# A hybrid attention and MoE block: fourteen instead of twelve column blocks of W_in beside the first norm's modulation

## The chip, the cores and the metric

The kernel runs on one core of a Trainium2 chip, all in float32. The time is the device time of one execution in microseconds (us); lower is better. Engines are named as the profile names them: PE (TensorE, with PEld for its weight loads), DVE (VectorE), ACT (ScalarE), POOL (GpSimd) and SP (SyncE, which here only issues loads).

## The reference

One layer on 256 tokens of width 2048, with a conditioning vector c:

```
mod = silu(c) @ w_ada + b_ada                  # sh1, sc1, gt1, sh2, sc2, gt2, 2048 wide each
h = modulate(rms_norm(x, g_mix), sh1, sc1)
qa, ka, va, qb, kb, vb = split(h @ w_in)       # 1024, 256, 256, 1024, 1024, 1024 columns
o_a = sliding-window attention of 16 heads (4 key heads, ALiBi, sinks)
o_b = chunked attention of 16 heads with a learned relative bias
x = x + gt1 * (concat(rms_norm(o_a), rms_norm(o_b)) @ w_out)
h = modulate(rms_norm(x, g_ffn), sh2, sc2)
x = x + gt2 * hier_moe(h)                      # 4 groups of 8 experts, top 1 group, top 2 experts
y = modulate(rms_norm(x, g_final), shf, scf)   # from silu(c) @ w_ada_final
```

All weights together are some 595 MB, read once.

## The kernel before

**The ring.** Every large weight goes through one ring of six buffers of 2 MB (`RING = 6`, class `Ring`). SP issues the loads in one fixed order. The load of a tile is issued when a buffer is free, so at most six tiles are on their way, waiting, or in use.

**First stage (four quarters q).** Quarter q holds four tiles of w_ada, 2 MB each (columns of sh1 and sc1), and two tiles of W_in's first 1536 columns, 1.5 MB each (`first_quarters`). PE does the w_ada products of quarter 0 and of the fourth tile of the other quarters (L314); DVE does the first three tiles of quarters 1 to 3 (L319, L321). The sums are transposed into columns (L329 to L338), the four chunks of hT are modulated (L342, L344), and then PE multiplies the chunks by ten blocks of 128 columns (qA and kA, L349) and by vA's 256 columns (L354). They add up over the quarters in six PSUM banks (`early`, `early_v`). One more PSUM bank ("m") and two of tag "t", which take the modulation sums and all transposes in turn, fill the eight.

**Second stage (`in_step`).** The remaining 3072 columns of W_in are six blocks of 512 columns: qB0, kB0, vB0, qB1, kB1, vB1. Each is two tiles of 8 chunks, so there are 12 steps of 2 MB (L575, L579). Between the PE tiles lie "vector tiles" in the ring: 2 MB of w_ada or w_ada_final, which DVE alone multiplies by silu(c) and adds up in four instructions each (`vec_step`, L383, L385). `VECTOR_TILES` says how many of the 44 lie behind each PE tile: 2 and 3 in turn over the twelve steps.

**Attention.** `weave(n)` is called twice per step: it starts the next n heads (`scores`: PE products, DVE maxima L475 and L476, ACT exponentials, DVE reciprocals L493, POOL scaling L494 and L495), transposes the heads of the call before (`turn`, L502) and multiplies those of the call before that by the values (`values`, L518). After each of a head's four phases it emits up to two instructions of vector tiles, if any are queued. The 16 heads of A come first. POOL makes a bias tile for each of them (L462).

**The order on each engine** is that in which the program emits instructions. The loop over the tiles is

```
    step = out_step(h, idx) if name == "wo" else in_step(name, h, idx)
    next(step)
    queue += [(*tile, kk) for tile in extra for kk in range(tile[2])]
    vec_steps(4)
    for _ in step:
        pass
    vec_steps()
```

`in_step` yields after each half of its tile: after the first half `weave(0)` has been called, after the second `weave(2)`.

**Third stage (`out_step`).** Eight tiles of w_out (L608): four for A's half, then, when all heads are through and B's norm (L536) is known, four for B's half, with the router between. `weave(1 + t)` is called after each of an A step's two token halves, so three heads can start in one step. Then 8 passes over four experts each take the 192 tiles of the MoE through the same ring (L819, L847).

Of the kernel before, what the change touches and what calls it, by code (L numbers as in the profile page):

```python
# [18 lines left out]
AF = mybir.ActivationFunctionType  # L19
# [16 lines left out]
NEG = -1e30  # L36
RING = 6

VECTOR_TILES = [2, 3, 2, 3, 2, 3, 2, 3, 2, 3, 2, 3, 2, 2, 2, 2, 3, 2, 1, 0]


ROW_ADA, ROW_FIN, ROW_MIX, ROW_FFN, ROW_GFIN, ROW_OA, ROW_OB = 0, 24, 32, 36, 40, 44, 46
# [42 lines left out]
def block_kernel(ctx: ExitStack, tc: tile.TileContext, a: dict):  # L85
# [7 lines left out]
    ring = Ring(nc, ringp, RING)  # L93
# [5 lines left out]
    def rows(w, row, n, col, width):  # L99

        return w[row : row + 128 * n, col : col + width].rearrange("(k p) n -> p k n", p=128)
# [3 lines left out]
    first_quarters = []  # L105
    for q in range(4):
        gemv = [ring.add((4, 2, 512), [rows(ada, 512 * i, 4, s * D + q * 512, 512) for s in range(2)]) for i in range(4)]
        first_quarters.append((gemv, [ring.add((2, 1536), rows(w_in, q * 512 + h * 256, 2, 0, 1536)) for h in range(2)]))

    vec_tiles = []  # L110
    for name, w, col in (("gt1", ada, 2 * D), ("sh2", ada, 3 * D), ("sc2", ada, 4 * D), ("gt2", ada, 5 * D), ("scf", fin, D), ("shf", fin, 0)):
        for c in (0,) if name == "shf" else (0, 1024):
            vec_tiles += [((name, c // 512), k, 4, 1024, rows(w, k * 512, 4, col + c, 1024)) for k in range(4)]
    blocks = [("qB0", 1536), ("kB0", 2560), ("vB0", 3584), ("qB1", 2048), ("kB1", 3072), ("vB1", 4096)]
    pe_tiles = [(name, h, rows(w_in, h * 1024, 8, col, 512)) for name, col in blocks for h in range(2)]
    pe_tiles += [("wo", h * 4 + n, rows(w_out, h * 1024, 8, n * 512, 512)) for h in range(2) for n in range(4)]
    order = []
    for (name, h, src), count in zip(pe_tiles, VECTOR_TILES):
        part = ring.add((8, 512), src)
        extra = [(vn, k, n, ring.add((n, width), vs)) for vn, k, n, width, vs in vec_tiles[:count]]  # L120
        del vec_tiles[:count]
        order.append((name, h, part, extra))
# [88 lines left out]
    with ExitStack() as sa:  # L211
# [4 lines left out]
        def bank(tag, name, bufs=2):  # L216
            return ps.tile([128, 512], F32, tag=tag, name=name, bufs=bufs)

        pc = bank("m", "pc", 1)
        PE.transpose(pc[:, 0:16], crow, ident[0:16, 0:16])  # L220
        ce = pa.tile([128, 16], F32, name="ce")
# [22 lines left out]
        G.dma_start(out=U, in_=rel[:, 0:UW])  # L244


        p0 = bank("t", "p0")
        p1 = bank("t", "p1")
        for q in range(4):
            PE.transpose(p0[:, q * 128 : (q + 1) * 128], pr[:, q * 128 : (q + 1) * 128], ident)  # L250
        for q in range(4):
# [49 lines left out]
        kS = bflat[:, 1024:1536].rearrange("p (c n) -> p c n", c=2)  # L301
        R["gt1"] = bflat[:, 3584:4096]
        for q, (gemv, parts) in enumerate(first_quarters):
            mods = bank("t", f"mods{q}")
            on_vector = gemv[:3] if q else []
            acc = pa2.tile([128, 1024], F32, tag="acc", name=f"acc_first{q}").rearrange("p (s n) -> p s n", s=2) if q else None
            for i, idx in enumerate(gemv):
                w = ring.get(idx)
                for k in range(4):
                    c = cact[:, 4 * i + k : 4 * i + k + 1]  # L310
                    if idx not in on_vector:
                        for s in range(2):
                            r = 64 * s + 32 * (k % 2)
                            PE.matmul(  # L314
                                mods[r : r + 32, :], lhsT=c.to_broadcast([128, 32]), rhs=w[:, k, s, :],
                                start=i == len(on_vector) and k < 2, stop=i == 3 and k > 1 and not (q and k == 2), skip_group_check=True,
                            )
                    elif i or k:
                        V.scalar_tensor_tensor(acc, w[:, k], c, acc, op0=ALU.mult, op1=ALU.add)  # L319
                    else:  # L320
                        V.tensor_scalar(acc, w[:, k], c, None, op0=ALU.mult)  # L321
                ring.release(idx)
                if q == 0 and i == 1:
                    turn_x()
                    early = [bank("w", "qA0"), bank("w", "qA1"), bank("s", "qA2"), bank("s", "qA3"), bank("v", "kA", 1)]
                    early_v = bank("m", "vA", 1)
            if q:
                for s in range(2):
                    PE.matmul(mods[64 * s : 64 * s + 32, :], lhsT=ones[:, 0:32], rhs=acc[:, s], start=False, stop=True, skip_group_check=True)  # L329
            row = oT_flat[:, 2048 + (q % 2) * 512 : 2560 + (q % 2) * 512]  # L330
            S.copy(row, mods)
            pt = bank("t", f"mod{q}")
            for c in range(4):
                PE.transpose(pt[:, c * 128 : (c + 1) * 128], row[:, c * 128 : (c + 1) * 128], ident)
            cols = small.tile([128, 2, 4], F32, tag="mod", name=f"mod{q}")
            V.tensor_reduce(cols, pt.rearrange("p (c s h r) -> p s c h r", c=4, s=2, h=2)[:, :, :, :, 0], axis=AX.X, op=ALU.add)
            V.tensor_tensor(cols, cols, bmod[:, :, q, :], op=ALU.add)
            V.tensor_tensor(cols[:, 1, :], cols[:, 1, :], gmix[:, q, :], op=ALU.mult)  # L338
            for c in range(4):
                k = 4 * q + c  # L340
                if c % 2:
                    S.activation(hT[:, k, :], hT[:, k, :], AF.Identity, bias=cols[:, 0, c : c + 1], scale=cols[:, 1, c : c + 1])  # L342
                else:
                    V.tensor_scalar(hT[:, k, :], hT[:, k, :], cols[:, 1, c : c + 1], cols[:, 0, c : c + 1], op0=ALU.mult, op1=ALU.add)  # L344
            for c in range(4):
                kk = 4 * q + c
                w = ring.get(parts[c // 2])[:, c % 2, :]
                for n in range(10):
                    PE.matmul(  # L349
                        early[n // 2][:, (n % 2) * 256 : (n % 2 + 1) * 256], lhsT=w[:, n * 128 : (n + 1) * 128], rhs=hT[:, kk, :],  # L350
                        start=kk == 0 and n % 2 == 0, stop=kk == 15, skip_group_check=True,
                    )
                for t in range(2):
                    PE.matmul(  # L354
                        early_v[:, t * 256 : (t + 1) * 256], lhsT=hT[:, kk, t * 128 : (t + 1) * 128], rhs=w[:, 1280:1536],
                        start=kk == 0 and t == 0, stop=kk == 15, skip_group_check=True,
                    )
                if c % 2:
                    ring.release(parts[c // 2])
# [3 lines left out]
        for s in range(4):  # L363
# [3 lines left out]
            else:  # L367
                V.tensor_scalar(dst, early[s], 0.125, None, op0=ALU.mult)
        V.tensor_copy(vA.rearrange("p t n -> p (t n)"), early_v)


        accs = {}
# [124 lines left out]

        def turn(kind, h):
            st = live.pop((kind, h))
            tp = bank("t", f"tp{kind}{h}")  # L500
            for i in range(3):
                PE.transpose(tp[:, i * 128 : (i + 1) * 128], st[:, i * 128 : (i + 1) * 128], ident)  # L502
            pt = pa2.tile([128, 384], F32, tag="pt", name=f"pt{kind}{h}")
            S.copy(pt, tp[:, 0:384])
            live["T", kind, h] = pt
# [59 lines left out]

        def in_step(name, h, idx):
            w = ring.get(idx)
            if h == 0:
                open_banks["b"] = [bank("w", f"pw_{name}{i}") for i in range(2)]
            b = open_banks["b"]  # L570
            for s in range(2):
                for k in range(8):
                    kk = 8 * h + k
                    if name[0] == "v":
                        PE.matmul(b[s], lhsT=hT[:, kk, s * 128 : (s + 1) * 128], rhs=w[:, k, :], start=kk == 0, stop=kk == 15)  # L575
                    else:
                        for n in range(2):
                            c = 2 * s + n
                            PE.matmul(  # L579
                                b[s][:, n * 256 : (n + 1) * 256], lhsT=w[:, k, c * 128 : (c + 1) * 128], rhs=hT[:, kk, :],  # L580
                                start=kk == 0 and n == 0, stop=kk == 15, skip_group_check=True,
                            )
                if s == 1:
                    ring.release(idx)
                if h == 1:
                    if name[0] == "v":
                        S.copy(half[name][:, s, :], b[s])
                    else:
                        dst, scale = dest[name]
                        S.activation(dst[:, 2 * s : 2 * s + 2, :].rearrange("p c n -> p (c n)"), b[s], AF.Identity, scale=scale)  # L590
                weave(2 * s)
                yield
# [32 lines left out]

        def router_turns(n):
            for c in range(2):
                tp = bank("t", f"x1t{n}{c}")
                hh = hflat[:, D + 1024 + c * 512 : D + 1024 + (c + 1) * 512].rearrange("p (j n) -> p j n", j=2)
                for j in range(2):  # L630
                    for t in range(2):
# [463 lines left out]
```

## Time and profile before

| what | value |
|---|---|
| median of 3 runs | 1508.13 us (1502.47, 1508.13, 1508.76) |
| profiled execution | 1504.53 us, its span 1502.9 us |
| PE / DVE / ACT / POOL busy | 79% / 33% / 11% / 10% of the span |
| moved from memory | 599.38 MB, mean 399 GB/s |
| mean granted PE clock | 0.913 of full speed |

The span runs from the first to the last instruction; 1.6 us of the profiled execution lie outside it. Busy time of PE is modelled, and shares are means over stages with different limits, so the stages have to be read one by one.

### The profile page before, as it was taken

To read this page: it belongs to the slowest core of one execution; us is meant where nothing else is said; L and a number is where in the kernel's file an instruction comes from. 1 tells how busy PE (TensorE), PEld (TensorE's weight loads), DVE (VectorE), ACT (ScalarE), POOL (GpSimd) and SP (SyncE) were. 2 spreads that over 40 slices of the span, in tenths; PEclk is the share of its full clock that TensorE was granted. 3 is DMA by queue.
4 is the path that set the end of the run, shared out by engine and by line. 5 is a ranking of instruction groups with operands and counts; after the bars stand their busy time and mean duration, and the time that the engine had idled before them with its cause. 6 is when DMAs were issued, how large, how long until landed. Compare 5 with 4: busy or idle time off the path is not lost.

```text
span 1502.9 us, 14247 instructions
## 1 busy us (share of the span) xinstructions
PE 1190.7 (79%) x5927; PEld 528.7 (35%) x5928; DVE 495.8 (33%) x803; ACT 167.4 (11%) x425; POOL 155.1 (10%) x144
## 2 busy tenths in 40 slices
PE   5898999999999987766677667767767757666877
PEld 2676875864444532222212212211211211221222
DVE  1453688877668520111111211111201201111113
ACT  2000222223221210000000100000100000000012
POOL 1000245532441100000000000000000000000002
PEclk9899999999999998889879989888989988898998
DMA  9999999999888999999999999999999999999995
GB/s 335 395 393 400 383 402 402 402 401 401 339 325 321 385 390 421 421 419 421 421 422 421 421 421 421 421 422 421 421 421 421 421 421 421 421 421 421 421 410 182
DMA packets 125469, 599.38 MB, mean 399 GB/s; under 512 B 5880, under 2 KB 8488, under 8 KB 78040
## 3 DMA queue, kind: packets, MB, share of 16 engines
q1 hardware_dynamic: 121248, 594.82, 98.0%
q10 hardware_dynamic: 4120, 3.57, 0.7%
q8 instruction: 48, 0.79, 0.2%
q14 instruction: 21, 0.17, 0.0%
q0 software_dynamic: 32, 0.02, 0.0%
HBM read 596.02 MB, written 2.12 MB: 398 GB/s over the span
## 4 chain that ended last, share of the span: by engine, by line
DMA 45%; PE 10%; DVE 0%; issue 0%; ACT 0%; ACTq 0%; SPq 0%; DVEq 0%
DMA ring<-w_up 22%; DMA ring<-w_down 12%; DMA ring<-w_gate 12%; PE up L819 4%; PE yp L847 3%; PE gp L819 2%; PE sc_g L866 1%; PE last L1050 0%; PE last L1049 0%; ACT big L1061 0%; DVE ys_g L860 0%; PE last L1060 0%; ACTq L1062 0%; DVE act_g L836 0%; PE sm_g L810 0%
## 5 line engine op out<-in xcount | busy, mean ns | idle before, releaser
L847 PE MATMUL yp<-ring,actT_g 128*32 128x512 f32 x1024 | 186.2, 784 | 102.9 <-DMA ring<-w_down 97.1
L819 PE MATMUL up<-ring,xg_g 128*32 128x512 f32 x1024 | 171.6, 701 | 78.2 <-DMA ring<-w_up 78.2
L819 PE MATMUL gp<-ring,xg_g 128*32 128x512 f32 x1024 | 169.2, 692 | 62.7 <-DMA ring<-w_gate 61.4
L868 DVE TENSOR_TENSOR x<-x,sc_g 128x512 f32<-128x512 f32 x64 | 44.0, 688 | 255.4 <-PE sc_g L866 255.4
L847 PEld LDWEIGHTS yp<-ring,actT_g 128*32 128x32 f32 x1024 | 40.0, 135 | 233.8 <-DMA ring<-w_down 135.2
L608 PE MATMUL po<-ring,oT 128*128 128x512 f32 x256 | 116.1, 609 | 0.5 <-DMA ring<-w_out 0.5
L789 DVE TENSOR_SCALAR xg_g<-g_g,gsc,sh2c 128x128 f32<-128x128 f32 x64 | 26.2, 409 | 257.9 <-PE g_g L780 240.6
L871 POOL TENSOR_TENSOR big<-x,xg_gscf 128x512 f32<-128x512 f32 x8 | 10.0, 1273 | 960.9 <-DVE x L868 960.9
L819 PEld LDWEIGHTS up<-ring,xg_g 128*32 128x32 f32 x1024 | 38.1, 124 | 197.5 <-DMA ring<-w_up 111.7
L819 PEld LDWEIGHTS gp<-ring,xg_g 128*32 128x32 f32 x1024 | 37.2, 122 | 180.5 <-DMA ring<-w_gate 90.4
L787 ACT ACTIVATE xg_g<-g_g,sh2c,gsc 128x128 f32<-128x128 f32 x64 | 29.3, 457 | 511.6 <-DVE xg_g L789 509.6
L860 DVE TENSOR_TENSOR ys_g<-yp,gt2bc 128x512 f32<-128x512 f32 x32 | 21.8, 690 | 174.1 <-PE yp L847 174.1
L385 DVE SCALAR_TENSOR_TENSOR acc_gt<-ring,cact,acc_gt 128x1024 f32<-128x1024 f32 x60 | 78.5, 1309 | 1.6
L608 PEld LDWEIGHTS po<-ring,oT 128*128 128x128 f32 x256 | 49.1, 196 | 61.3 <-issue 59.8
L780 PEld LDWEIGHTS g_g<-pn_g,big 128*128 128x128 f32 x512 | 59.6, 192 | 28.0 <-issue 27.2
L349 PE MATMUL qA<-hT,ring 128*128 128x256 f32 x256 | 64.6, 410 | 4.8 <-DVE hT L344 3.5
L780 PE MATMUL g_g<-pn_g,big 128*128 128x128 f32 x512 | 65.6, 281 | 1.4 <-DVE pn_g L772 1.4
L866 PE MATMUL sc_g<-ys_g,smat_g 128*128 128x512 f32 x128 | 64.6, 628 | 1.6 <-DVE ys_g L860 1.6
L349 PEld LDWEIGHTS qA<-hT,ring 128*128 128x128 f32 x256 | 52.7, 207 | 14.2 <-DVE hT L344 4.3
L579 PE MATMUL pw_kB<-hT,ring 128*128 128x256 f32 x256 | 57.0, 382 | 0.0
L575 PE MATMUL pw_vB<-ring,hT 128*128 128x512 f32 x128 | 56.5, 597 | 0.0
L579 PE MATMUL pw_qB<-hT,ring 128*128 128x256 f32 x256 | 56.5, 381 | 0.0
(328 smaller groups left out, 1126.6 us busy)
## 6 DMA issues: line engine op xcount, KB each, us to landing
ring<-w_gate SPq DMA_DIRECT2D x64, 2048.0 KB, 20.3
ring<-w_up SPq DMA_DIRECT2D x64, 2048.0 KB
ring<-w_down SPq DMA_DIRECT2D x62, 2048.0 KB, 22.0
ring<-w_ada SPq DMA_DIRECT2D x32, 2048.0 KB, 15.8
ring<-w_ada SPq DMA_DIRECT2D x32, 1024.0 KB, 14.1
ring<-w_ada_final SPq DMA_DIRECT2D x16, 2048.0 KB, 10.9
ring<-w_in SPq DMA_DIRECT2D x12, 2048.0 KB, 16.3
ring<-w_out SPq DMA_DIRECT2D x8, 2048.0 KB
```

The source lines that it names most:

```text
L349: PE.matmul(early[n // 2][:, (n % 2) * 256 : (n % 2 + 1) * 256], lhsT=w[:, n * 128 : (n + 1) * 128], rhs=hT[:, kk, :], start=kk == 0 and n ...
L385: V.scalar_tensor_tensor(accs[name], w[:, kk, :], cact[:, c : c + 1], accs[name], op0=ALU.mult, op1=ALU.add)
L575: PE.matmul(b[s], lhsT=hT[:, kk, s * 128 : (s + 1) * 128], rhs=w[:, k, :], start=kk == 0, stop=kk == 15)
L579: PE.matmul(b[s][:, n * 256 : (n + 1) * 256], lhsT=w[:, k, c * 128 : (c + 1) * 128], rhs=hT[:, kk, :], start=kk == 0 and n == 0, stop=kk = ...
L608: PE.matmul(b, lhsT=oT[:, (i // 4) * 8 + k, t * 128 : (t + 1) * 128], rhs=w[:, k, :], start=k == 0, stop=k == 7)
L780: PE.matmul(pm[:, i * 128 : (i + 1) * 128], lhsT=big[:, t, kk * 128 : (kk + 1) * 128], rhs=pn[:, t, :], start=t == 0 and i == 0, stop=t == ...
L787: S.activation(xg[:, kk, :], pm[:, i * 128 : (i + 1) * 128], AF.Identity, bias=sh2c[:, kk : kk + 1], scale=gsc2[:, kk : kk + 1])
L789: V.tensor_scalar(xg[:, kk, :], pm[:, i * 128 : (i + 1) * 128], gsc2[:, kk : kk + 1], sh2c[:, kk : kk + 1], op0=ALU.mult, op1=ALU.add)
L819: PE.matmul(bankt[32 * e : 32 * e + 32, :], lhsT=xg[:, kk, 32 * e : 32 * e + 32], rhs=w[e // 2][:, e % 2, j, :], start=kk == 0, stop=kk == ...
L847: PE.matmul(y[32 * e : 32 * e + 32, :], lhsT=aT[:, fc, 32 * e : 32 * e + 32], rhs=w(e)[:, n * 512 : (n + 1) * 512], start=fc == 0, stop=fc ...
L866: PE.matmul(pm, lhsT=sm[:, t * 128 : (t + 1) * 128], rhs=ys[:, n, :], start=True, stop=True)
L868: V.tensor_tensor(x1[:, t, c], x1[:, t, c], pm, op=ALU.add)
```

## The change

The two W_in tiles of each quarter become 1792 columns wide (1.75 MB), and PE multiplies each chunk by two more blocks: columns 1536 to 1791, which are the first half of qB0. Their sums stand in a seventh bank, "t1"; the modulation sums of this stage use "t0" alone, and later transposes take t0 and t1 in turn (`tbank`). The other half of qB0 is one tile of 16 chunks of 256 columns (rows of 1 KB), done in one step that has one `weave(2)` and one yield at its end. So there are 11 steps in place of 12, and `VECTOR_TILES` gives them 3, 3, 2 in turn.

```diff
-VECTOR_TILES = [2, 3, 2, 3, 2, 3, 2, 3, 2, 3, 2, 3, 2, 2, 2, 2, 3, 2, 1, 0]
+VECTOR_TILES = [3, 3, 2, 3, 3, 2, 3, 3, 2, 3, 3, 2, 2, 2, 2, 3, 2, 1, 0]
...
-        first_quarters.append((gemv, [ring.add((2, 1536), rows(w_in, q * 512 + h * 256, 2, 0, 1536)) for h in range(2)]))
+        first_quarters.append((gemv, [ring.add((2, 1792), rows(w_in, q * 512 + h * 256, 2, 0, 1792)) for h in range(2)]))
...
-    blocks = [("qB0", 1536), ("kB0", 2560), ("vB0", 3584), ("qB1", 2048), ("kB1", 3072), ("vB1", 4096)]
-    pe_tiles = [(name, h, rows(w_in, h * 1024, 8, col, 512)) for name, col in blocks for h in range(2)]
+    blocks = [("kB0", 2560), ("vB0", 3584), ("qB1", 2048), ("kB1", 3072), ("vB1", 4096)]
+    pe_tiles = [("qB0", 0, rows(w_in, 0, 16, 1792, 256))]
+    pe_tiles += [(name, h, rows(w_in, h * 1024, 8, col, 512)) for name, col in blocks for h in range(2)]
...
-        part = ring.add((8, 512), src)
+        part = ring.add((16, 256) if name == "qB0" else (8, 512), src)
...
+        def tbank(name):
+            turns[0] += 1
+            return bank(f"t{turns[0] % 2}", name, 1)
...
-            mods = bank("t", f"mods{q}")
+            mods = bank("t0", f"mods{q}", 1)
...
+                    early_b = bank("t1", "qB", 1)
...
-            pt = bank("t", f"mod{q}")
+            pt = bank("t0", f"mod{q}", 1)
...
-                for n in range(10):
+                for n in (*range(10), 12, 13):
                     PE.matmul(
-                        early[n // 2][:, (n % 2) * 256 : (n % 2 + 1) * 256], lhsT=w[:, n * 128 : (n + 1) * 128], rhs=hT[:, kk, :],
+                        (early + [None, early_b])[n // 2][:, (n % 2) * 256 : (n % 2 + 1) * 256], lhsT=w[:, n * 128 : (n + 1) * 128], rhs=hT[:, kk, :],
...
+        S.activation(oT[:, 8:10, :].rearrange("p c n -> p (c n)"), early_b, AF.Identity, scale=0.125)
...
-            tp = bank("t", f"tp{kind}{h}")
+            tp = tbank(f"tp{kind}{h}")
...
             w = ring.get(idx)
+            if name == "qB0":
+                b = bank("w", "pw_qB0")
+                for kk in range(16):
+                    for n in range(2):
+                        PE.matmul(
+                            b[:, n * 256 : (n + 1) * 256], lhsT=w[:, kk, n * 128 : (n + 1) * 128], rhs=hT[:, kk, :],
+                            start=kk == 0 and n == 0, stop=kk == 15, skip_group_check=True,
+                        )
+                ring.release(idx)
+                S.activation(half[name][:, 2:4, :].rearrange("p c n -> p (c n)"), b, AF.Identity, scale=0.125)
+                weave(2)
+                yield
+                return
```

## Rows read from the trace of the kernel before

**Rows 1.** The page, section 4: the chain that ended last, by engine.

```profile
DMA 45%; PE 10%; DVE 0%; issue 0%; ACT 0%; ACTq 0%; SPq 0%; DVEq 0%
```

**Rows 2.** Windows: length, engines' busy us (instructions), granted PE clock, DMA share, GB/s.

```profile
45.00:130.00 85.00, 77.08 (x355) 59.05 (x355) 48.37 (x51) 5.03 (x9) 0.00 (x0) 0.96 1.04 395
...
128.80:134.00 5.20, 5.16 (x16) 4.23 (x17) 0.31 (x1) 0.67 (x2) 0.00 (x0) 0.67 1.05 390
...
213.00:361.00 148.00, 148.00 (x660) 94.70 (x658) 118.65 (x201) 41.23 (x127) 60.49 (x53) 1.00 1.03 402
361.00:546.00 185.00, 173.44 (x615) 81.37 (x614) 122.55 (x211) 36.94 (x104) 53.18 (x45) 0.97 0.91 353
666.00:1447.00 781.00, 552.12 (x3056) 166.66 (x3059) 118.53 (x182) 35.26 (x73) 0.00 (x0) 0.88 1.01 421
```

**Rows 3.** Timeline of PE, first stage: start, length in us, ..., [idle before <-releaser].

```profile
49.38 3.62 PE L349 MATMUL qA<-hT,ring 128*128 128x256 f32 x16
...
54.56 3.62 PE L349 MATMUL qA<-hT,ring 128*128 128x256 f32 x16
...
65.01 1.92 PE L314 MATMUL mods<-ring,cact 128*32 128x512 f32 x16
...
70.31 5.41 PE L349 MATMUL qA<-hT,ring 128*128 128x256 f32 x16 [1.19 <-DVE hT L344]
...
92.92 1.04 PE L314 MATMUL mods<-ring,cact 128*32 128x512 f32 x2
...
99.52 3.72 PE L349 MATMUL qA<-hT,ring 128*128 128x256 f32 x16 [1.18 <-DVE hT L344]
...
119.48 1.03 PE L354 MATMUL vA<-ring,hT 128*128 128x256 f32 x4
...
123.52 1.49 PE L314 MATMUL mods<-ring,cact 128*32 128x512 f32 x11 [1.59 <-DMA ring<-w_ada]
...
128.84 5.41 PE L349 MATMUL qA<-hT,ring 128*128 128x256 f32 x16 [1.18 <-DVE hT L344]
```

**Rows 4.** Timeline of PE, second stage.

```profile
151.36 13.98 PE L579 MATMUL pw_qB<-hT,ring 128*128 128x256 f32 x64
...
181.65 14.08 PE L579 MATMUL pw_kB<-hT,ring 128*128 128x256 f32 x64
195.66 0.66 PE L518 MATMUL opA<-ptA,big 128*64 128x256 f32 x4
...
198.14 7.17 PE L579 MATMUL pw_kB<-hT,ring 128*128 128x256 f32 x32
```

**Rows 5.** Timeline of DVE, start of the second stage.

```profile
152.94 6.57 DVE L385 SCALAR_TENSOR_TENSOR acc_gt<-ring,cact,acc_gt 128x1024 f32<-128x1024 f32 x5
168.02 0.29 DVE L475 CUSTOM_DVE_ANT_0 stA<-spA,biasA 128x128 f32<-128x128 f32 x1 [8.50 <-POOL biasA L462]
...
169.77 2.60 DVE L385 SCALAR_TENSOR_TENSOR acc_gt<-ring,cact,acc_gt 128x1024 f32<-128x1024 f32 x2
...
172.73 0.17 DVE L493 RECIPROCAL denA<-denA 128x2 f32<-128x2 f32 x1
```

**Rows 6.** Timeline of POOL, the same stretch.

```profile
166.84 0.20 POOL L454 MEMSET biasB<- 64x128 f32 x1 [3.11 <-DMA biasB<-scratch]
```

**Rows 7.** Loads: KB each, us from issue to landing.

```profile
ring<-w_ada SPq DMA_DIRECT2D x32, 2048.0 KB, 15.8
...
x<-x SPq DMA_DIRECT2D x1, 2048.0 KB, 8.4
```

**Rows 8.** Timeline of PE, third stage.

```profile
361.65 7.13 PE L608 MATMUL po<-ring,oT 128*128 128x512 f32 x16 [0.50 <-DMA ring<-w_out]
...
452.94 0.71 PE L536 MATMUL pnB<-ones,sqB 128*128 128x1 f32 x4 [3.11 <-POOL sqB L529]
```

**Rows 9.** Waits of PE between 350 and 460 us: total us, times, longest.

```profile
PE tpB L502 <- POOL stB L495: 2.1, 4, 0.6
PE tpB L502 <- POOL stB L494: 2.1, 2, 1.5
```

More of the change, by code (lines that the diff above doesn't have):

```diff
@@ L217, in bank @@
             return ps.tile([128, 512], F32, tag=tag, name=name, bufs=bufs)
+        turns = [0]
+        def tbank(name):
+            turns[0] += 1
+            return bank(f"t{turns[0] % 2}", name, 1)
         pc = bank("m", "pc", 1)
@@ L244, in block_kernel @@
         G.dma_start(out=U, in_=rel[:, 0:UW])
-        p0 = bank("t", "p0")
-        p1 = bank("t", "p1")
+        p0 = tbank("p0")
+        p1 = tbank("p1")
         for q in range(4):
@@ L627, in router_turns @@
             for c in range(2):
-                tp = bank("t", f"x1t{n}{c}")
+                tp = tbank(f"x1t{n}{c}")
                 hh = hflat[:, D + 1024 + c * 512 : D + 1024 + (c + 1) * 512].rearrange("p (j n) -> p j n", j=2)
```

## The prediction

> **What bounds the kernel now.** I read the chain of the page first, then the windows by stage, then the timelines of PE and DVE where the change sits. The chain puts 45% of the span on loads and 10% on PE [rows 1], but it is followed back from the end and lies in the MoE almost wholly, so the earlier part must be read from the windows. From 666 us to 1447 us loads run at 421 GB/s and PE has slack [rows 2]: whatever delays the start of the MoE is added to the end, for its 192 tiles can hardly come faster. From 361 to 546 us PE is busy 173.4 of 185 us and loads fall to 353 GB/s: PE sets the pace, and the ring is full behind it. From 45 to 361 us both are nearly full: loads at 395 to 402 GB/s, PE 77.1 of 85 us in the first stage and 148 of 148 in most of the second [rows 2]. Which of the two decides shows where they meet: PE starts the first w_out product at 361.65 us after waiting 0.50 us for its load [rows 8]. So that load's landing is one fixed post, and what PE still owes behind it is the other. My sum goes by these two.
>
> **First stage.** Each of 16 chunks gets two more blocks, four instructions. A chunk is 24 instructions and its pitch is 54.56 - 49.38 = 5.18 us [rows 3], so 64 more cost 64 x 0.216 = 13.8 us, 3.45 us in a quarter. Against that, loads grow by 0.524 MB in a quarter, 1.33 us at 395 GB/s [rows 2]. PE thus falls behind its loads by 2.1 us more in each quarter, and its waits on them go. From the end of one quarter's W_in work to the next one's start PE took 70.31 - 65.01 = 5.3 us where loads were in time, 99.52 - 92.92 = 6.6 and 128.84 - 120.5 = 8.3 where they were late [rows 3]; the last two fall to 5.3, which gives back 4.3 us. The stage's end moves from 151.36 to 151.36 + 13.8 - 4.3 = 160.9 us. Unknown is where the clock falls: one quarter began its W_in work with 16 products in 3.72 us, two with 5.41 [rows 3], behind a wait and at a granted clock of 0.67 [rows 2]; so +/- 1.8 us.
>
> **qB0's rest.** 64 instructions in place of 128: 14.0 us [rows 4], to 174.9 us. One pair of heads less has been started by then; a pair's whole turn (values, transposes, scores) costs PE 198.14 - 195.66 = 2.5 us [rows 4], a debt that is paid later. The scores that are left here I put at a third of it, 0.9 us. So kB0 starts at 175.8, against 181.65 [rows 4]: 5.9 us earlier.
>
> Rows of 1 KB in its load, 7 KB instead of 6 KB before it: loads run at 395 GB/s where rows of 2 KB prevail and at 421 with the MoE's 8 KB [rows 2]. If halving the rows once more cost as much again, this one tile would take 0.3 us longer; PE comes to it late anyway, so I count nothing. The Trainium skill (DMA: Bandwidth & Descriptors, Specifications) puts line rate at transfers of 512 B and more, by which the tile would lose nothing; no run here shows rows of 1 KB, and its rule alone doesn't explain 395 against 421.
>
> **The vector tiles behind qB0 are where I expect the loss.** Before, the step yields after half a tile, the loop then queues the vector tiles and emits four DVE instructions ahead of the first heads' maxima. The trace shows this order kept: products of the first two tiles from 152.94 us on, then DVE stands idle for 8.50 us until POOL's bias, and the two products that were emitted behind the maxima come only at 169.77, behind them [rows 5]. The new step yields only after weave(2). So the maxima and reciprocals of heads 0 and 1 are emitted ahead of every vector tile, and weave's own vec_steps find an empty queue. DVE does nothing on the ring until those heads are through.
>
> When is that? Before, the first maximum ran 168.02 - 151.36 = 16.7 us after the stage's end [rows 4, 5], held by POOL, which waited for the bias's load until 166.84 [rows 6]. The same distance gives 160.9 + 16.7 = 177.6 us; bounded below by the scores alone, 175.9. From there to the last reciprocal it took 172.9 - 168.0 = 4.9 us with 2.6 us of vector products between [rows 5]; without them between 2.3 and 4.9, I take 3.6. So the first vector tile starts at 181.2, not near 152, and ends four products of 1.3 us [rows 5] later, at 186.4.
>
> Meanwhile the ring fills: qB0, its three vector tiles, kB0's first tile and one more vector tile take the six buffers. The next load waits for qB0's release at 174.9, the one behind it for the first vector tile, 186.4. With the queue run dry a 2 MB load takes 8.4 us, as that of x did alone [rows 7] (least 5.2, a tile at 402 GB/s; most 15.8, the median of w_ada's 2 MB loads in a full queue [rows 7]): it lands at 194.8. From this tile to the first of w_out I count 34 tiles of 2.097 MB in the new order, 5.22 us each at 402 GB/s: 177.5 us. It lands at 372.3 instead of 361.65, **+10.7 us**. Nothing between can make that up, since loads run at their rate already. PE doesn't hold it back: ten steps from 175.8 at the old pace (361.65 - 181.65 = 180.0 us) end at 355.8.
>
> Bounds: scores in place of the bias, 2.3 us, and a load of 5.2 us give 188.6 and +4.4 us; the slower clock (+1.8), 4.9 us and 15.8 us give 205.3 and +21.1. (The Trainium skill's same page, Anatomy of one DMA, fits 2.0 us plus bytes at 436 GB/s to a load issued by POOL; taken over as an estimate that is 6.8 us for such a tile, and the sum would be 1.6 us less. The 8.4 us of x disagree, and stand.)
>
> **Third stage.** PE is the bound, so what it owes adds: the pair of heads, 2.5 us. The heads now end in the fourth w_out step instead of the third, so one pair more is transposed right behind a 7 us block, and waits for POOL as such pairs do: 4.2 us in two places [rows 9], so 0 to 2.1, I take 1.1. Before B's half the last head's values follow its transposes directly, with ACT's copy between, some 0.6 us; the wait for B's norm, 3.11 us [rows 8], was there before. Together **+4.2 us**, at most 7 with one more fall of the clock. Bank turns, the extra ACT copy and wider tiles cost nothing: one copy of 0.6 us on an engine that is 11% busy, and t0 and t1 alternate as the two buffers did.
>
> **Sum.** 1504.5 + 10.7 + 4.2 = 1519.4 us against the profiled execution, with 1511 to 1533 as this case's own range. The three runs lie 2.1 us below to 4.2 us above that execution; for that I add 1.5 us: 1521.
>
> **Rivals.** (1) The hole stays hidden: DVE's tiles are taken up earlier than I read, or the loads queued cover it. Then w_out still lands at 361.65, since its bytes ahead are the same, and only the third stage's debt stays: 1507 to 1510. For it: the median load stood 15.8 us in its queue [rows 7]; against it: six buffers are all there is, and DVE's 8.50 us idle with work behind it. (2) Not slower: PE was the bound all along and the 0.50 us at 361 us chance. Then the 5.9 us count, less the 2.5: -3.4, 1501 us; with the 2.5 us covered too 1499. It decides only if the loads from 45 to 361 us gain 2% (5.9 of 317 us); their share is at 1.03 to 1.04 of the engines already [rows 2], so I doubt it. (3) Worse: DVE, 29 us late, stays late for the heads too, PE's transposes wait in each of ten steps and the clock falls 1.8 us with some of these waits; with 1 us each more, +12 on top: 1533.
>
> **Chances.** My case 0.60, rival 1 0.14, rival 2 0.12, rival 3 0.14. About 0.5%, 7.5 us, is what a measurement of this kernel can tell from none. I count half of rival 2 as faster, for what its two numbers may be short of: 0.06. Same is its other half, rival 1, and a tenth of my case at its low end: 0.26. Slower is the rest of my case and rival 3: 0.68. The range 1506 to 1534 leaves out rival 2 and the upper part of rival 3.
>
> **What will show it.** PE's first stage ends near 161 us and kB0 starts near 176 (wrong if 165: no waits were won back). DVE has no vector product between the stage's end and 180 us, and loads fall well below 395 GB/s between 165 and 195 us; if they don't, my main step is wrong. Between 200 and 372 us PE waits for W_in's tiles. The first w_out product starts near 372 us, and the MoE's first some 15 us later than before. Wrong would make it above all that the loads' gap is shorter than 11 us, or that PE has more room in the third stage than its busy share says.

## The result, and the profile after

The changed kernel takes 1525.34 us, median of five runs (1521.42 to 1528.21), against 1508.13 us, median of five (1502.47 to 1509.59): 1.0124 times the time of before, 95% interval 1.0104 to 1.0144. Ratios here and below are estimated from the runs of both kernels and are not quotients of the medians, which here would give 1.0114. It is slower by 17 us where 13 were forecast. Of all runs in this document one was in a slow state and is left out of its kernel's ratio: 2123.78 us, of x6 below, whose nine others took 1496.54 to 1500.61. The profiled execution is the slowest of its five runs (1528.21 us, span 1526.6); that of before lies 3.6 us under its own median, so the two traces differ by 23.7 us, 6.5 more than the medians.

Four posts cut the span. PE's first product of qB0's own tile ends the first stage: 151.36 us before [rows 4], 160.85 after. The first w_out product starts at 361.65 before [rows 8] and 374.66 after, +13.0. From there to the first product of B's half of w_out it takes 91.86 before and 104.12 after, +12.3. From that to the MoE's first product it takes 89.2 and 89.65, and what follows is 2 us shorter. The whole loss thus lies between the end of the first stage and B's half of w_out, in two places.

**The first place is the hole in the loads.** Windows (length, busy us of PE, PEld, DVE, ACT and POOL with instructions, granted clock, DMA share, GB/s), three of the kernel after and then two of the kernel before:

```profile
165.00:195.00 30.00, 26.22 (x132) 22.17 (x130) 17.47 (x27) 4.97 (x14) 9.65 (x10) 0.97 0.67 248
195.00:235.00 40.00, 37.00 (x146) 23.66 (x148) 36.14 (x54) 8.81 (x31) 14.42 (x11) 0.89 1.04 403
...
175.60:374.70 199.10, 186.30 (x807) 125.75 (x806) 164.96 (x266) 48.02 (x153) 74.79 (x63) 0.95 1.01 392
```

```profile
165.00:195.00 30.00, 30.00 (x150) 25.64 (x149) 25.30 (x45) 6.42 (x24) 16.92 (x14) 1.00 1.03 392
...
181.60:361.70 180.10, 179.60 (x815) 120.15 (x813) 148.05 (x254) 48.37 (x153) 75.54 (x63) 1.00 1.03 402
```

Loads fall to 248 GB/s for 30 us and are back at 403 behind it; before, the same 30 us moved 392 GB/s. 144 GB/s for 30 us are 4.3 MB, two tiles, 10.8 us of loading at 402 GB/s. The timeline of DVE (start, length, ..., idle before and its releaser) shows where they stop:

```profile
161.05 0.69 DVE L378 COPY big<-vA 128x512 f32<-128x512 f32 x1 [2.70 <-PE vA L363]
175.83 0.29 DVE L485 CUSTOM_DVE_ANT_0 stA<-spA,biasA 128x128 f32<-128x128 f32 x1 [14.09 <-PE spA L480]
...
179.24 0.17 DVE L503 RECIPROCAL denA<-denA 128x2 f32<-128x2 f32 x1
179.32 0.81 DVE L393 TENSOR_SCALAR acc_gt<-ring,cact 128x1024 f32<-128x1024 f32 x1
180.16 19.90 DVE L395 SCALAR_TENSOR_TENSOR acc_gt<-ring,cact,acc_gt 128x1024 f32<-128x1024 f32 x15
```

Before, vector products stood right behind the stage's end, at 152.94 [rows 5]. Now DVE does nothing for 14.09 us, since the first heads' maxima were emitted ahead of the vector tiles; behind the heads it runs 20.7 us without a gap over vector tiles. Four products make a tile, so by these rows the first is through at about 184.1 us and the second at 189.4. SP's queue shows the next load of W_in held until the second of them is through:

```profile
161.04 23.53 SPq L72 DMA_DIRECT2D ring<-w_ada  x3
189.52 0.37 SPq L72 DMA_DIRECT2D ring<-w_in  x1
```

PE meets that load (timeline of PE, rows of W_in's products):

```profile
160.85 13.98 PE L582 MATMUL pw_qB<-hT,ring 128*128 128x256 f32 x64
...
175.62 14.08 PE L602 MATMUL pw_kB<-hT,ring 128*128 128x256 f32 x64
...
198.00 16.82 PE L602 MATMUL pw_kB<-hT,ring 128*128 128x256 f32 x64 [6.78 <-DMA ring<-w_in]
...
255.95 14.05 PE L602 MATMUL pw_qB<-hT,ring 128*128 128x256 f32 x64 [1.96 <-DMA ring<-w_in]
...
292.41 8.78 PE L602 MATMUL pw_kB<-hT,ring 128*128 128x256 f32 x32 [2.45 <-DMA ring<-w_in]
...
302.10 7.17 PE L602 MATMUL pw_kB<-hT,ring 128*128 128x256 f32 x32
...
313.06 7.17 PE L602 MATMUL pw_kB<-hT,ring 128*128 128x256 f32 x32 [0.84 <-DMA ring<-w_in]
```

Two things are to be seen. The waits (6.78, 1.96, 2.45, 0.84) come one after another over 120 us, each when PE has caught up with loads that stay late. And a block behind a wait can cost more than the wait alone: 16.82 in place of 14.08 us, 8.78 in place of 7.17. In the stretch from kB0 to w_out PE is busy 186.30 of 199.10 us, where before it was 179.60 of 180.10: 12.3 us more of idle time and 6.7 more busy, at a granted clock of 0.95 in place of 1.00, together 19.0; kB0's earlier start, 6.0, goes off: +13.0.

**The second place is the third stage**, in the same timeline of PE:

```profile
374.66 7.03 PE L631 MATMUL po<-ring,oT 128*128 128x512 f32 x16
383.85 0.33 PE L512 MATMUL tpB<-ident,stB 128*128 128x128 f32 x1 [1.36 <-POOL stB L504]
...
388.44 8.54 PE L631 MATMUL po<-ring,oT 128*128 128x512 f32 x16
...
411.50 0.33 PE L512 MATMUL tpB<-ident,stB 128*128 128x128 f32 x1 [2.67 <-POOL stB L504]
...
416.08 8.38 PE L631 MATMUL po<-ring,oT 128*128 128x512 f32 x16
...
439.52 0.33 PE L512 MATMUL tpB<-ident,stB 128*128 128x128 f32 x1 [1.53 <-POOL stB L504]
...
443.65 8.24 PE L631 MATMUL po<-ring,oT 128*128 128x512 f32 x16
```

Three pairs of heads wait for POOL in place of two [rows 9], 8.7 us in all with the short waits between, against 4.2. Waits of PE from 355 to 485 us in the kernel after (total us, times, longest):

```profile
PE tpB L512 <- POOL stB L504: 5.6, 3, 2.7
PE tpB L512 <- POOL stB L505: 3.1, 6, 0.6
```

Each of the three is followed by a w_out block of 8.2 to 8.5 us instead of 7.0 to 7.1 [rows 8]. Before, that holds for the second of the two pairs and not for the first, whose wait was shorter:

```profile
370.21 0.33 PE L502 MATMUL tpB<-ident,stB 128*128 128x128 f32 x1 [0.62 <-POOL stB L494]
...
373.80 7.13 PE L608 MATMUL po<-ring,oT 128*128 128x512 f32 x16
...
394.29 0.33 PE L502 MATMUL tpB<-ident,stB 128*128 128x128 f32 x1 [1.51 <-POOL stB L494]
...
398.87 8.73 PE L608 MATMUL po<-ring,oT 128*128 128x512 f32 x16
```

Windows of the kernel after around its first pair, columns as above:

```profile
384.00:388.00 4.00, 3.00 (x10) 1.69 (x9) 0.00 (x0) 0.96 (x2) 4.00 (x5) 0.56 1.05 396
388.00:397.00 9.00, 9.00 (x20) 3.63 (x20) 6.11 (x10) 0.99 (x4) 3.22 (x3) 0.82 0.98 393
```

The granted clock is 0.56 of 2.4 GHz, a mean near its lower level of 1.2, in the stretch with the transposes that wait, and 0.82 in that of the block behind. Over the whole way to B's half:

```profile
374.00:479.00 105.00, 92.61 (x285) 41.84 (x284) 67.25 (x118) 28.43 (x83) 46.52 (x43) 0.92 0.78 297
```

### The profile page after: what moved, and what is told of

Same layout as the page of the kernel before. It is cut to its first block, busy times and chain, and to the rows that moved or that the text cites. A ratio compares the mean times of both kernels' runs of the same rounds, so it can differ in the third digit from the quotient of the medians.

```text
span 1526.6 us, 14245 instructions
## 1 busy us (share of the span) xinstructions
PE 1201.3 (79%) x5927; PEld 536.4 (35%) x5928; DVE 495.7 (32%) x803; ACT 168.0 (11%) x425; POOL 151.1 (10%) x144
## 4 chain that ended last, share of the span: by engine, by line
DMA 57%; PE 37%; DVE 2%; POOL 1%; issue 1%; ACT 1%; SPq 0%; ACTq 0%; POOLq 0%; DVEq 0%
DMA ring<-w_down 26%; DMA ring<-w_gate 12%; DMA ring<-w_up 12%; PE po L631 6%; PE yp L870 5%; PE qA L358 4%; PE pw_vB L598 3%; DMA ring<-w_in 3%; PE gp L842 3%; PE up L842 3%; PE pw_kB L602 2%; PE pw_qB L602 2%; DMA biasB<-scratch 2%; DMA ring<-w_ada 2%; PE pw_qB L582 1%; PE vA L363 1%
## 5 line engine op out<-in xcount | busy, mean ns | idle before, releaser
L870 PE MATMUL yp<-ring,actT_g 128*32 128x512 f32 x1024 | 179.2, 749 | 105.2 <-DMA ring<-w_down 99.4
L842 PE MATMUL gp<-ring,xg_g 128*32 128x512 f32 x1024 | 177.5, 730 | 69.0 <-DMA ring<-w_gate 68.5
L602 PE MATMUL pw_kB<-hT,ring 128*128 128x256 f32 x256 | 63.5, 413 | 10.1 <-DMA ring<-w_in 10.1
L602 PEld LDWEIGHTS pw_kB<-hT,ring 128*128 128x128 f32 x256 | 53.0, 210 | 20.6 <-DMA ring<-w_in 8.4
```

Of the source, the lines that this page charges most:

```text
L602: PE.matmul(b[s][:, n * 256 : (n + 1) * 256], lhsT=w[:, k, c * 128 : (c + 1) * 128], rhs=hT[:, kk, :], start=kk == 0 and n == 0, stop=kk = ...
L842: PE.matmul(bankt[32 * e : 32 * e + 32, :], lhsT=xg[:, kk, 32 * e : 32 * e + 32], rhs=w[e // 2][:, e % 2, j, :], start=kk == 0, stop=kk == ...
L870: PE.matmul(y[32 * e : 32 * e + 32, :], lhsT=aT[:, fc, 32 * e : 32 * e + 32], rhs=w(e)[:, n * 512 : (n + 1) * 512], start=fc == 0, stop=fc ...
```

## The experiments

Theory: (a) the order on DVE opens the hole and costs what w_out is late; (b) the heads that are moved into the third stage cost the rest, through waits for POOL's scaling and the clock behind them. Rivals: the change's other parts (the wider tiles, rows of 1 KB, banks used singly) cost part of it; and for (b), that the third stage is late because of the hole. Posts of each profiled execution, us:

| kernel | median | ratio to before, interval | first stage ends | first w_out | to B's half | to the MoE |
|---|---|---|---|---|---|---|
| before | 1508.13 | 1 | 151.36 | 361.65 | 91.86 | 89.21 |
| after | 1525.34 | 1.0124 (1.0104 to 1.0144) | 160.85 | 374.66 | 104.12 | 89.65 |
| x1 | 1515.67 | 1.0045 (1.0029 to 1.0062) | 161.02 | 361.92 | 105.29 | 88.01 |
| x2 | 1515.11 | 1.0056 (1.0035 to 1.0077) | 158.55 | 365.46 | 95.74 | 89.11 |
| x3 | 1514.27 | 1.0051 (1.0035 to 1.0068) | 149.80 | 368.44 | 92.01 | 89.05 |
| x4 | 1513.79 | 1.0054 (1.0036 to 1.0073) | 149.70 | 361.74 | 102.88 | 87.63 |
| x5 | 1495.01 | 0.9927 (0.9898 to 0.9956) | 151.21 | 361.40 | 83.44 | 90.85 |
| x6 | 1499.32 | 0.9955 (0.9937 to 0.9973) | 159.84 | 361.25 | 85.99 | 90.07 |
| x7 | 1498.03 | 0.9947 (0.9932 to 0.9961) | 149.61 | 361.28 | 85.99 | 87.62 |
| x8 | 1504.61 | 0.9985 (0.9967 to 1.0003) | 149.68 | 363.99 | 97.11 | 89.33 |
| x9 | 1505.40 | 0.9988 (0.9975 to 1.0001) | 156.58 | 369.49 | 85.98 | 89.33 |
| x10 | 1493.65 | 0.9897 (0.9881 to 0.9912) | 157.57 | 368.12 | 67.26 | 95.43 |
| x11 | 1495.46 | 0.9913 (0.9900 to 0.9927) | 149.67 | 361.39 | 83.45 | 90.77 |

x1 to x4, x5 to x8 and x9 to x11 were each timed on another chip, beside runs of the kernel before on that chip (medians 1507.4, 1505.24 and 1508.11), so between these groups the ratios are compared. A post is read from one execution.

**x1: the changed kernel with qB0's vector tiles emitted ahead of its heads.**

```diff
+            if name == "qB0":
+                queue += [(*tile, kk) for tile in extra for kk in range(tile[2])]
+                vec_steps()
             next(step)
-            queue += [(*tile, kk) for tile in extra for kk in range(tile[2])]
+            if name != "qB0":
+                queue += [(*tile, kk) for tile in extra for kk in range(tile[2])]
```

> The changed kernel, but qB0's three vector tiles are queued and all their twelve DVE products emitted ahead of its step, so ahead of the maxima of heads 0 and 1; nothing else differs. Theory (order of emission): DVE takes the tiles up at about 162 us instead of 179, the loads' gap from 165 to 195 us closes, kB0's second tile is there when PE comes to it (no wait of 6.8 us), and the first w_out product starts at 361 to 364 us instead of 374.7. The third stage still has two heads more than before, some 12 us by the trace of the changed kernel (from 193.8 us between the first w_out product and the MoE's first one, against 181.1), so the total is 10 to 14 us over the kernel before: ratio 1.007 to 1.009. Rival (the single 16-chunk tile of qB0 is given back late, or its 1 KB rows load slowly): the wait at kB0's second tile stays at 5 us or more, w_out starts at 370 us or later, ratio 1.011 to 1.014.

DVE's products run from 161.82 us, the loads keep their rate and w_out starts at its old time. DVE's timeline and the window of the hole:

```profile
161.82 0.74 DVE L393 TENSOR_SCALAR acc_gt<-ring,cact 128x1024 f32<-128x1024 f32 x1
162.60 14.52 DVE L395 SCALAR_TENSOR_TENSOR acc_gt<-ring,cact,acc_gt 128x1024 f32<-128x1024 f32 x11
```

```profile
165.00:195.00 30.00, 30.00 (x150) 25.58 (x149) 24.69 (x42) 7.21 (x24) 10.41 (x10) 1.00 1.03 397
```

The third stage stays as long as in the changed kernel, so it is not the hole that makes it late. The order alone takes the ratio from 1.0124 to 1.0045, 12 us, with some 4 us of uncertainty from the two intervals; the 1.007 to 1.009 that were expected were too shy.

**x3: the converse, the order alone in the kernel before** (qB0's first step runs to its end before its vector tiles are queued).

```diff
             next(step)
+            if name == "qB0" and h == 0:
+                for _ in step:
+                    pass
             queue += [(*tile, kk) for tile in extra for kk in range(tile[2])]
```

> The kernel before with the suspected order alone: the first step of qB0 runs to its end, heads 0 and 1 with it, before its vector tiles are queued. Theory (order of emission): DVE starts on the first vector tile at about 172 us instead of 152, the load that waits for it and all behind it come 10 to 20 us later, loads fall clearly below 395 GB/s between 165 and 190 us, PE waits for kB0's or vB0's tiles and starts w_out 4 to 12 us after 361.7. Ratio 1.003 to 1.008. Rival (the order costs nothing, queued loads cover it): w_out starts at 361 to 363 us and the ratio is 0.998 to 1.002.

DVE and PE of this kernel:

```profile
166.39 0.29 DVE L475 CUSTOM_DVE_ANT_0 stA<-spA,biasA 128x128 f32<-128x128 f32 x1 [15.69 <-POOL biasA L462]
...
169.89 0.80 DVE L383 TENSOR_SCALAR acc_gt<-ring,cact 128x1024 f32<-128x1024 f32 x1
```

```profile
183.06 15.74 PE L579 MATMUL pw_kB<-hT,ring 128*128 128x256 f32 x64 [2.89 <-DMA ring<-w_in]
```

Loads from 160 to 185 us run at 274 GB/s (389 before), PE waits, w_out starts 6.8 us later, and the third stage does not move. With none of the change's tiles, blocks or banks in it, the order costs 0.51%, 8 us.

**x2: x1, with one head more started in each of qB1's two steps**, so that 24 are started before w_out, as in the kernel before.

```diff
-                weave(2 * s)
+                weave(1 if name == "qB1" and s == 0 else 2 * s)
```

> As the kernel with the tiles first, and the two heads that are owed are started earlier: one more in each of qB1's two steps, after the first half of the tile. Theory: PE comes to the first w_out product some 5 us ahead of its load in that kernel, so the two heads are free there; w_out still starts at 361 to 365 us, and the third stage takes 180 to 184 us as before. Total within 4 us of the kernel before: ratio 0.998 to 1.003. Rival (the third stage is longer for another reason than the two heads, such as the order of its vector tiles): the third stage stays at 190 us or more and the ratio at 1.006 or more.

The third stage gets 9.5 us shorter, as (b) has it, but w_out starts 3.5 us later, with PE's transposes waiting for POOL in the second stage instead (1.7 us in four waits, and a W_in tile 2.2 us). The time is a miss: 1.0056, no better than x1's 1.0045, where 0.998 to 1.003 were expected. Its profiled run is the fastest of its four (1510.03 of 1510.03 to 1516.88), so where the others lost their time was not seen. By this trace two heads are not free in the second stage either.

**x4: the kernel before with one pair of heads less by kB0.**

```diff
-                weave(2 * s)
+                weave(0 if name == "qB0" and h == 0 else 2 * s)
```

> The kernel before, but no heads are started in the first step of qB0, so 22 instead of 24 are through their scores when w_out begins. Theory (the two owed heads make the third stage longer, by their work, by the waits for POOL of pairs transposed 7 us after their scores, and by the clock that falls with the waits): w_out starts at 360 to 362 us and the stage to the MoE's first product grows from 181.1 to 190 to 194 us: ratio 1.006 to 1.008. By the sum in the prediction the stage grows by 4.2 us only: ratio 1.003. Rival (the third stage grows through the late loads, not the heads): no growth, ratio 1.000.

w_out starts as before, and the way to B's half grows by 11.0 us, with three pairs waiting in place of two. Two of the waits and the block behind one:

```profile
370.98 0.33 PE L502 MATMUL tpB<-ident,stB 128*128 128x128 f32 x1 [1.40 <-POOL stB L494]
...
397.67 0.33 PE L502 MATMUL tpB<-ident,stB 128*128 128x128 f32 x1 [2.47 <-POOL stB L494]
...
402.25 8.34 PE L608 MATMUL po<-ring,oT 128*128 128x512 f32 x16
```

So a moved pair costs about what the changed kernel lost there, and the forecast's +4.2 us was too small. x3 and x4, each one cause alone, cost 0.51% and 0.54%; their sum is 1.05% of the 1.24%, and the rest is within the intervals. x4 also stands beside x1: both start two heads fewer and have their tiles first, and only x1 has the wider tiles, the rows of 1 KB and the single banks. Their ratios, 1.0054 and 1.0045, show no cost of these parts, and no gain.

**x5, x11: the kernel before with the heads' scaling on ACT**, to take POOL away from in front of the transposes (x11 is the same kernel again).

```diff
-            G.tensor_scalar(st[:, 0:128], st[:, 0:128], den[:, 0:1], None, op0=ALU.mult)
-            G.tensor_scalar(st[:, 128:384], st[:, 128:384], den[:, 1:2], None, op0=ALU.mult)
+            S.activation(st[:, 0:128], st[:, 0:128], AF.Identity, scale=den[:, 0:1])
+            S.activation(st[:, 128:384], st[:, 128:384], AF.Identity, scale=den[:, 1:2])
```

> The kernel before with the heads' two scalings by 1/den moved from POOL to ACT. Theory (pairs that are transposed 7 us after their scores wait for POOL's scaling, and the clock falls behind these waits): PE's 4.2 us of waits for POOL in the third stage shrink below 1.5 us, A's half of w_out (361.7 to 453.5 us before, 91.9 us) takes 85 to 89 us, w_out still starts at 361 to 362 us. Ratio 0.995 to 0.998. Rival (the waits only move, to ACT behind its exponentials): A's half stays at 91 us or more, ratio 0.999 to 1.003.

> The kernel before with the scalings on ACT once more, beside the one with four heads earlier, for a narrower interval: 1493 to 1497 us, ratio 0.990 to 0.994, w_out at 361 to 362 us and A's half 82 to 85 us.

The waits for POOL's scaling are gone, and up to the norm of B no w_out block takes over 7.13 us. The gain is larger than expected (0.9927 for 0.995 to 0.998). PE's timeline up to the norm of B, and two windows, of x5 and then of the kernel before:

```profile
361.40 7.13 PE L608 MATMUL po<-ring,oT 128*128 128x512 f32 x16 [0.40 <-DMA ring<-w_out]
370.93 7.13 PE L608 MATMUL po<-ring,oT 128*128 128x512 f32 x16
...
443.97 1.01 PE L536 MATMUL pnB<-ones,sqB 128*128 128x1 f32 x4 [3.12 <-POOL sqB L529]
```

```profile
361.00:445.00 84.00, 79.65 (x262) 36.83 (x262) 64.05 (x101) 30.64 (x90) 22.40 (x17) 0.99 0.99 381
```

```profile
361.00:454.00 93.00, 84.15 (x262) 38.17 (x262) 63.91 (x101) 23.27 (x70) 41.21 (x37) 0.96 0.90 345
```

The same 262 products take 84.15 busy us before and 79.65 here: of the 9.0 us between the windows, 4.5 are waits and 4.5 slower products, at a granted clock of 0.96 in place of 0.99.

**x6, x7 and x9: the same edit in x1, in x4 and in the changed kernel itself.**

> The changed kernel with qB0's vector tiles ahead of its step, and the scalings on ACT. Theory: w_out starts at 361 to 363 us (the loads set it), A's half of w_out takes 89 to 95 us instead of 105.3 with the tiles first alone, because the waits of three pairs for POOL and the clock's falls go and the work of two heads stays. Ratio 0.998 to 1.002. Rival: A's half stays above 100 us, ratio 1.004 or more.

> The kernel before with two heads fewer started before w_out, and the scalings on ACT. Theory: against the kernel before with the scalings on ACT alone, A's half of w_out is longer by the two heads' own work and the longer drain, 2.5 to 5 us, not by the 11 us that two heads fewer cost with the scalings on POOL. Ratio 0.998 to 1.001. Rival (the 11 us are not the waits for POOL): 8 us or more, ratio 1.003 or more.

> The changed kernel with the scalings on ACT and nothing else: the order of emission alone is left as a cause. Theory: DVE takes up qB0's vector tiles at about 179 us, the loads' gap from 165 to 195 us stays, w_out starts at 370 to 375 us, A's half takes 86 to 89 us, and the time is 9 to 13 us over the changed kernel with the tiles first and the scalings on ACT: 1507 to 1512, ratio 1.001 to 1.005. Rival (the late start of w_out came from the heads' waits and the clock, not from the loads): w_out starts at 365 us or earlier, ratio 0.996 to 0.999.

x6 and x7 came out faster than expected (0.9955 for 0.998 to 1.002, 0.9947 for 0.998 to 1.001), as x5 had. Without POOL in the way, the pair of heads costs 85.99 - 83.44 = 2.55 us (x7 against x5), which is the 2.5 us that the prediction gave for its work. x6 against x7 is the comparison of x1 with x4 once more: 0.08% between them, so the wider tiles and the other parts of the change show no cost here either. The changed kernel's third stage falls from 104.12 to 85.98 us in x9, with the hole still in it. The hole stands alone in x9 against x6, and PE shows it as in the changed kernel:

```profile
193.25 11.94 PE L602 MATMUL pw_kB<-hT,ring 128*128 128x256 f32 x47 [6.30 <-DMA ring<-w_in]
```

w_out starts 8.2 us later than in x6, the spans of the two profiled executions differ by 7.9 us, and the ratios by 0.33%, 5 us. The ratio, 0.9988, is under the 1.001 to 1.005 that were expected, and the hole costs less than the 12 us between the changed kernel and x1. In the traces the difference is the first stage: x9's ended 4.3 us earlier than the changed kernel's with the same instructions, at a granted clock of 0.99 in place of 0.94 from 0 to 150 us, and from its end to w_out both take about as long, 212.9 and 213.8 us. What the hole costs in the mean over executions stays open; the three comparisons (the changed kernel with x1, x3 with before, x9 with x6) give 12, 8 and 5 us, each with some 2 to 4 us of uncertainty.

The window of x6 from w_out to B's half has the changed kernel's work in 19 us less:

```profile
361.20:447.20 86.00, 82.51 (x283) 38.24 (x281) 65.90 (x114) 36.89 (x107) 23.00 (x19) 1.00 0.96 369
```

**x8: the kernel before with its banks used singly** (`tbank` and t0 and t1 alone).

```diff
...
-            tp = bank("t", f"tp{kind}{h}")
+            tp = tbank(f"tp{kind}{h}")
...
```

> The kernel before with the transposes' two PSUM banks as two tags of one buffer each, as in the change, and nothing else of it. Theory: nothing, since the two are taken in turn as before and the modulation sums' next use of their bank comes after its last reader anyway: ratio 0.998 to 1.002, first stage's end at 150 to 152 us. Rival (a transpose now waits for its bank): waits of PE for ACT's copies appear at the transposes, ratio above 1.003.

Nothing that could be measured. Its profiled run is the slowest of its ten, with 6.2 us of waits for POOL in the third stage against 4.2 before. As its median shows no such loss, that stage seems to vary by some us between executions, and one trace is not enough for a term of a few us. The way to B's half is 91.86 to 97.11 us in the four traces with two waiting pairs (before, x2, x3, x8) and 102.88 to 105.29 in the three with three (after, x1, x4).

**x10: x6 with one head more started in each of the four steps of qB1 and kB1**, so 26 before w_out in place of 22.

```diff
-                weave(2 * s)
+                weave(1 if name in ("qB1", "kB1") and s == 0 else 2 * s)
```

> The changed kernel with the tiles first, the scalings on ACT, and one head more in each of qB1's and kB1's four steps, so 26 heads are started before w_out instead of 22. Theory: where the loads set w_out's start, four heads (5 us of PE) are free before it and missing behind it: w_out at 361 to 364 us, A's half 80 to 83 us, 1491 to 1495 us in all, ratio 0.990 to 0.993. Rival (PE has no time left before w_out, as its start without a wait at 361.25 us in the kernel without these heads suggests): w_out at 365 to 368 us, A's half 81 to 83, the total as without these heads, 1497 to 1500, ratio 0.994 to 0.997.

w_out starts at 368.12 us, later than expected (361 to 364), and the way to B's half is much shorter (67.26 for 80 to 83), since the heads are through early and the norm of B is waited for no more:

```profile
428.15 7.03 PE L631 MATMUL po<-ring,oT 128*128 128x512 f32 x16
435.02 0.50 PE L546 MATMUL pnB<-ones,sqB 128*128 128x1 f32 x4
435.38 13.98 PE L631 MATMUL po<-ring,oT 128*128 128x512 f32 x32
```

Part of it goes back in B's half (95.43 us); the total is as expected. This is the fastest version, 1493.65 us (1492.55 to 1494.78), beside 1495.46 (1495.08 to 1496.55) for the kernel before with the scaling on ACT, on the same chip. With the order mended, the scaling on ACT and the four heads moved, the change is thus some 2 us ahead of the scaling on ACT alone; without the moved heads it is behind it (x6 0.9955, x5 0.9927). Nearly all the gain is the scaling's, and whether the kernel before would win as much by moving heads was not run.

## Why the prediction was right, and where it was off

- **First stage, 160.9 us: 160.85.** The waits for loads went as forecast: from one quarter's W_in work to the next PE took 5.30, 5.34 and 5.35 us. The exact hit is luck: the same stage ended at 156.58 to 161.02 in x1, x2, x6, x9 and x10. In the changed kernel, as before, two of the last three quarters began at the slower 5.41 us; in x9 all three took 3.72. The +/- 1.8 us for the clock was short by 2.5 on one side.
- **qB0's rest, kB0 at 175.8: 175.62.** The 64 products took 13.98 us. The cost of rows of 1 KB was not measured by itself; x1 and x6, which have them, start w_out at 361.92 and 361.25, so none is seen there.
- **The first maximum, 177.6: 175.83**, the lower bound: the scores decide, not POOL's bias. The bias was there at 170.72, 9.9 us behind the stage's end where before it took 15.5 [rows 6]; its small load, issued at 161.34, came sooner while the other loads ran dry, though that this is why was not tested. This takes 1.9 us off the rest of the chain: first vector tile 179.3 for 181.2.
- **The load that comes late.** The sum had kB0's second tile one load behind 194.8, at 200.0; PE starts on it at 198.00, 8.5 us after its issue, for 8.4. The Trainium skill (DMA: Bandwidth & Descriptors, Anatomy of one DMA) has a fit for loads issued by POOL, 2.0 us plus bytes at 436 GB/s, from which 6.8 us would be the estimate for such a tile; the trace stands nearer to x's row.
- **w_out, +10.7 us: +13.0, by another last link.** The sum had PE at w_out by 355.8, waiting there for the load. PE doesn't wait there: it came late itself, because it had met the late loads in W_in's tiles already, 12.1 us of waits, and lost 6.7 more to the clock. "Ten steps at the old pace" is the step that failed; it left out that a hole in the ring reaches PE at the next tile and not at the last. That both ways end within 2.3 us of each other is luck. Nothing won it back, as forecast; x1, x3 and x9 show the order as the cause.
- **Third stage, +4.2 us, at most 7: +12.3. This is the mis-sized term.** The pair's work was right (2.55 us). What was wrong is the wait: the forecast took 1.1 us, half of one place's, and at most one fall of the clock. PE is busy 82.51 of 86.00 us in x6's window and 92.61 of 105.00 in the changed kernel's: 8.9 us more of waits and 10.1 of slower products. The kernel before has 4.5 and 4.5 (x5). So the waits together already cost about twice their length, and a third pair brings some 10 us (x4: +11.0; 6 to 13 between the traces with two and with three pairs). x4 and x7 together show it: the heads are the same, and only what scales them differs.
- **The total.** Both terms came out larger, +25.3 us for 14.9 between the traces. The MoE gave back 2 us, and 6.5 us are how the two profiled runs stand to their medians, for which 1.5 had been added. So the two terms together were 10.4 us short and the total only 4.3, and that is luck too.
- **The rivals.** The hole is not hidden (248 GB/s) and PE gains nothing from its head start (x1 and x6 start w_out at the old time, though kB0 starts earlier). Rival 3 was right in its form, waits with the clock falling behind them, but not in its place: PE waits for late loads in the second stage, and for POOL only in the third.

## What to carry to other kernels

Where an engine takes its instructions in the order of the program, look at what stands behind its next wait: 14 us of DVE waiting for scores, with ready tiles behind, held the buffers of a ring, emptied the queue of loads and cost 5 to 12 us by the three comparisons, though DVE is busy a third of the time. Short waits of PE are to be counted with the slower products behind them, which here doubled them. Work that is moved to another stage brings the waits of that stage along, so price it by a row of the place where it lands.

## What the runs showed of the hardware

- Behind a wait of only 1.36 us, in a stretch of short transposes and waits of about 0.5 us, the granted clock was 0.56 (384 to 388 us of the kernel after), and behind the three pairs' waits of 1.36 to 2.67 us 16 products took 8.2 to 8.5 us, not 7.0 to 7.1. The seven traces of this document that have such pairs waiting hold 17 of them: behind the first waits of 0.62 (before) and 0.82 us (x3) the next 16 products took 7.13 us, behind the other 15, of 1.06 to 2.67 us, 8.24 to 9.90.
- A 2 MB load that SP issued at 174.9 us in the kernel after, with no other load on its way, took 8.8 us to land.
- POOL is slow at scaling a head's scores. The kernel before's POOL and then x5's ACT, grouped by line (instructions, busy us, mean ns):

```profile
L495 POOL TENSOR_SCALAR stA<-stA,denA 128x256 f32<-128x256 f32 x16 | 27.9, 1742 | 0.0
...
L495 POOL TENSOR_SCALAR stB<-stB,denB 128x256 f32<-128x256 f32 x16 | 16.9, 1056 | 0.0
```

```profile
L495 ACT ACTIVATE stA<-stA,denA 128x256 f32<-128x256 f32 x16 | 7.9, 493 | 0.0
L495 ACT ACTIVATE stB<-stB,denB 128x256 f32<-128x256 f32 x16 | 7.9, 493 | 0.0
```

The same instruction took POOL 1742 ns for A's heads and 1056 for B's; why it differs was not tried.
